# The convolution branch's output projection by seven products of quarters, with its operand's sums formed earlier

## The chip, the cores and the metric

The kernel is one launch on one core of a Trainium2 chip. The metric is the device time of that launch in microseconds (us), the median of several runs; lower is better. The engines are named as in the profile: PE is TensorE, which multiplies matrices, and PEld its loading of weights; DVE is VectorE; ACT is ScalarE; POOL is GpSimd and SP is SyncE, which here do little besides issuing DMA transfers. SBUF is the memory on the core, PSUM the eight banks that the matmuls write to, DRAM the memory off the core.

## The reference

One layer of a hybrid decoder in float32, with 512 tokens, width 2048, 1024 convolution channels, 1024 attention channels in 8 heads, and a hidden width of 8192:

```python
h = rmsnorm(x, g_mix)
z = h @ w_in                          # conv B | C | V, attn Q | K | V, forget, gate conv, gate attn
conv_y = cb * causal_dwconv(cc * cv, conv_w)          # 512 x 1024
conv_branch = conv_y @ w_conv_out                     # 512 x 2048
attn_branch = forgetting_attention(q, k, v, log_f) @ w_attn_out
merged = sigmoid(gate_c + b) * conv_branch + sigmoid(gate_a + b) * attn_branch
x = x + merged @ w_mix_out
h = rmsnorm(x, g_mlp)
x = x + square(relu(h @ w_ff1)) @ w_ff2
out = rmsnorm(x, g_final)
```

The change concerns the product that makes `conv_branch`.

## The kernel before

Every float32 operand is split in two: `hi`, which ACT copies into the type that PE multiplies (L100), and `lo`, the rest, which DVE subtracts (L101). A product is then three matmuls: hi by hi, hi by lo, lo by hi.

The large projections do with seven products of quarters what plainly takes eight (the Strassen-Winograd scheme): `Group` (L170 to L312) cuts the operands into quarters A11, A12, A21, A22, forms sums of the other operand S1 to S4 once for all groups, and sums of the weights for each group by `sub` (L104). `whole` runs the products A11, A12, S1, S3, S2, S4, A22 in this order into PSUM banks a, b, a, c, d; `snap` (ACT) copies a bank into a tile `o`, `plus` (DVE, L107) adds another bank to it, and `put` stores the result. A matmul there is 128x128 by 128x256. A product has six matmuls for each tile of 128 rows that the quarter has in depth: 48 in a group of `w_in`. A group's last argument, `extra`, puts a surplus matmul of 192 columns at the head of a named product: "first" (L137) or in a spare bank (L631).

The work up to the end of attention and its place in time: the columns of `w_in` for K, Q and V come first, then six z groups (the convolution's B, C and V, stored in DRAM as `z_d`), the first four among the attention heads. The last two z groups start at 482.1 and 521.1 us. `conv_job(f)`, for f from 0 to 7, loads three rows of `z_d`, forms u = C V and the three taps on DVE (L616, L619, L621, L622) and stores the result as `y_d` from POOL; DVE works on them from 474.6 to 602 us, in between the instructions of the groups. Eight gates groups follow on PE, up to 867.5 us; they store sigmoids of gates in `g_d`. `yact` and `aact` (`split_from`) load `y_d` and `a_d` (attention's output) and split them into SBUF.

The output projections come next, in `gemm_t` (L334): for a block c of 512 columns, conv with `yact`, then attn with `aact`, for c from 0 to 3. Each loads 1 MB of weights twice, splits them, and runs 96 matmuls of 128x128 by 128x512 into four banks, `pt`; `cons_cv` multiplies a bank by its gate into `held`, `cons_at` does so with the other, adds `held`, and splits the sum into `M`, the operand of mix_out, which follows at 1041.6 us. Then come ff1 (1222 to 1830 us) and ff2 (to the end).

What stands in an engine's queue is decided when the program is built: each engine runs its instructions in one fixed order, and an instruction that waits holds up all behind it. SP's and POOL's queues of DMA issues behave the same. Small tiles of the stage `pb` (`at`) share six buffers of 128x512; tiles `o` five; weights of groups four slots x0 to x3; `th` and `tl` (the split weights) two each.

Of the kernel before, what the change touches and what calls it, by code (L numbers as in the profile page):

```python
# [20 lines left out]
HS = S // 2  # L21
CW = D // 2
CT = CW // P
# [14 lines left out]
WBUF, SHIFT, PAD = 33 * 64, 16, 16  # L38
# [7 lines left out]
def tile_hybrid_block(ctx: ExitStack, tc, x, g_mix, w_in, b_f, b_gate, conv_w, w_conv_out,  # L46
                      w_attn_out, w_mix_out, g_mlp, w_ff1, w_ff2, g_final, out):
    nc = tc.nc
    x, out = x[0], out[0]
    w_in, w_conv_out, w_attn_out, w_mix_out = w_in[0], w_conv_out[0], w_attn_out[0], w_mix_out[0]  # L50
# [25 lines left out]
    z_d = dram.tile([3, CT, P, S], F32, name="z_d")  # L76
    g_d = dram.tile([2, KT, P, S], F32, name="g_d")
    y_d = dram.tile([CT, P, S], F32, name="y_d")
    a_d = dram.tile([CT, P, S], F32, name="a_d")
    x1_d = dram.tile([NT, P, D], F32, name="x1_d")  # L80
    s_d = [dram.tile([P, 2, 4, 7, HS], F32, name=f"s_d{i}") for i in range(DFF // 1024)]
# [17 lines left out]
    def split(src, hi, lo):  # L99
        nc.scalar.activation(out=hi, in_=src, func=AF.Copy)  # L100
        nc.vector.tensor_tensor(out=lo, in0=src, in1=hi.bitcast(F32), op=ALU.subtract)  # L101

    def sub(out, a, b):
        nc.vector.tensor_tensor(out=out, in0=a, in1=b, op=ALU.subtract)  # L104

    def add(out, a, b):
        nc.vector.tensor_tensor(out=out, in0=a, in1=b, op=ALU.add)  # L107
# [58 lines left out]
    def moving(t):  # L166

        return lambda q: (t[:, 0, q, :], t[:, 1, q, :])


    free, later = [0, 1, 2, 3], []

    class Group:
# [3 lines left out]
        def __init__(self, view, c1, c2, w, ST, mm, banks, put, scale=1.0, extra={}):  # L177
            self.extra = extra
            self.view, self.cs, self.w, self.ST, self.mm, self.banks = view, (c1, c2), w, ST, mm, banks
            self.put, self.scale, self.at = put, scale, {}  # L180

        def load(self, i, j):

            t = main.tile([P, KT // 2, self.w], F32, tag=f"x{free[0]}", name=f"x{i}{j}")
# [7 lines left out]
            return [bank(i, which) for i in self.banks["abcd".index(which)]]  # L192

        def run(self, ps, n, src, first):
            hi, lo = parts([P, KT // 2, self.w], SHIFT if self.w == HS else 0)
# [28 lines left out]
        def done(self, *ij):  # L224
            free.append(self.at.pop(ij))
# [90 lines left out]
    def eights(t, w=S):  # L316

        return tuple(t[:, e].rearrange("p (k s) -> p k s", s=w) for e in range(2))
# [11 lines left out]
    def slot(slots):  # L330
        turns[0] += 1
        return slots[turns[0] % len(slots)]

    def gemm_t(view, kt, c0, act, banks, consume, slots=(0, 3, 2)):  # L334

        ps = [bank(i, "pt") for i in banks]
        for k0 in range(0, kt, 4):
            hi, lo = wchunk(view, k0, c0, slot(slots))
            for j in range(4):
                js = slice(j * P, (j + 1) * P)  # L340
                for q in range(4):
                    k = k0 + q
                    xh, xl = act(k)
                    nc.tensor.matmul(ps[j], hi[:, q, js], xh, start=k == 0, stop=False)
                    nc.tensor.matmul(ps[j], hi[:, q, js], xl, start=False, stop=False)  # L345
                    nc.tensor.matmul(ps[j], lo[:, q, js], xh, start=False, stop=k == kt - 1)
        for j in range(4):
            consume(j, ps[j])
# [30 lines left out]
    class Quarters:  # L379
# [20 lines left out]
        def put(self, n, src, ts=slice(0, HS)):  # L400
            split(src[:, :, ts], self.ST[n][:, 0, :, ts], self.ST[n][:, 1, :, ts])
# [33 lines left out]
    ph = ExitStack()  # L435
# [3 lines left out]
    for t in range(NT):  # L439
        h = xp[t // 2][:, t % 2]  # L440
        n = 4 if t == 0 else 2
# [59 lines left out]
    def whole(g):  # L501
        g.head(True)
        g.tail2()
# [106 lines left out]
    def conv_job(f):  # L610
        cv, cc, cb = at("cv"), at("cc"), at("cb")
        for k, t in enumerate((cb, cc, cv)):
            nc.sync.dma_start(out=t, in_=z_d[k, f])
        u = at("u", [P, S + 2])
        nc.gpsimd.memset(u[:, 0:2], 0.0)
        nc.vector.tensor_tensor(out=u[:, 2:], in0=cv, in1=cc, op=ALU.mult)  # L616
# [5 lines left out]
        nc.vector.tensor_tensor(out=y, in0=cb, in1=y, op=ALU.mult)  # L622
        nc.gpsimd.dma_start(out=y_d[f], in_=y)
# [22 lines left out]
    for f in range(CT):  # L646
        conv_job(f)

    for f in range(0, KT, 2):
        def put_g(i, j, v, f=f):  # L650
            for b in range(2):
# [5 lines left out]
                    extra=apart(4, "S2", 0)))  # L657
# [21 lines left out]
    M = {}  # L679
    M[0, 0], M[0, 1], M[1, 0] = (eights(pair(i, F32R, "m"), HS) for i in (4, 5, 6))  # L680
    M[1, 1] = eights(pc_.tile([P, 2, D], F32R, tag="h", name="m"), HS)
    for c in range(4):
        held = main.tile([P, 4, S], F32, tag="x1", name="held")

        def gate(k, j, c=c):
            t = otile([P, S], "gt")
            nc.sync.dma_start(out=t, in_=g_d[k, 4 * c + j])
            return t

        def cons_cv(j, ps, held=held, gate=gate):  # L690
            g = gate(0, j)
            nc.vector.tensor_tensor(out=held[:, j, :], in0=ps, in1=g, op=ALU.mult)

        def cons_at(j, ps, held=held, gate=gate, c=c):
            g = gate(1, j)
# [174 lines left out]
    held = []  # L870
# [305 lines left out]
```

## Time and profile before

| | |
|---|---|
| median of 3 runs | 2461.55 us (2460.36 to 2463.54) |
| the profiled execution's own time | 2459.11 us |
| its span in the trace | 2457.4 us |
| granted clock of PE, mean | 0.998 |
| PE busy | 2431.6 us, 99% of the span, 16928 matmuls |
| PEld busy | 2247.3 us, 91% |
| DVE busy | 1921.1 us, 78% |
| ACT busy | 1149.1 us, 47% |
| POOL busy | 180.0 us, 7% |
| output projections (tile `pt`) | 867.5 to 1041.6 us |

The page has the span in us; its groups give busy time and the mean duration of one instruction in ns. A row of the trace by tile or line gives minimum, median and maximum duration in ns, the first and last start in us and the shapes. Durations of successive instructions on an engine overlap, so the distance between their starts is what counts for a sum.

### The profile page before, as it was taken

To read this page: it belongs to the slowest core of one execution; us is meant where nothing else is said; L and a number is where in the kernel's file an instruction comes from. 1 tells how busy PE (TensorE), PEld (TensorE's weight loads), DVE (VectorE), ACT (ScalarE), POOL (GpSimd) and SP (SyncE) were. 2 spreads that over 40 slices of the span, in tenths; PEclk is the share of its full clock that TensorE was granted. 3 is DMA by queue.
4 is the path that set the end of the run, shared out by engine and by line. 5 is a ranking of instruction groups with operands and counts; after the bars stand their busy time and mean duration, and the time that the engine had idled before them with its cause. 6 is when DMAs were issued, how large, how long until landed. Compare 5 with 4: busy or idle time off the path is not lost.

```text
span 2457.4 us, 39283 instructions
## 1 busy us (share of the span) xinstructions
PE 2431.6 (99%) x16928; PEld 2247.3 (91%) x16928; DVE 1921.1 (78%) x1592; ACT 1149.1 (47%) x1147; POOL 180.0 (7%) x280
## 2 busy tenths in 40 slices
PE   8999999999999999999999999999999999999998
PEld 8999999999999988888899999999998888888886
DVE  7887777788777744425688898988988888889898
ACT  6443443334444532225556666666665333333334
POOL 0100000001000000000000000000011001100000
PEclk9999999999999999999999999999999999999999
DMA  7564544456534554335645646556488576655662
GB/s 249 182 191 143 165 128 138 155 168 210 163 118 149 176 180 142 128 137 190 204 144 202 237 178 228 198 201 235 172 298 299 169 253 223 239 187 184 246 224 102
DMA packets 272036, 463.00 MB, mean 188 GB/s; under 512 B 10269, under 2 KB 172181, under 8 KB 271733
## 3 DMA queue, kind: packets, MB, share of 16 engines
q1 hardware_dynamic: 235136, 303.13, 38.3%
q0 software_dynamic: 35856, 156.25, 16.9%
q8 instruction: 133, 2.18, 0.4%
q10 hardware_dynamic: 868, 1.10, 0.1%
q14 instruction: 43, 0.34, 0.0%
HBM read 368.16 MB, written 92.27 MB: 187 GB/s over the span
## 4 chain that ended last, share of the span: by engine, by line
PE 95%; DVE 3%; issue 1%; ACT 1%; DMA 1%; POOL 0%; SPq 0%; DVEq 0%; POOLq 0%; ACTq 0%
PE a L148 6%; PE a L144 6%; PE a L146 6%; PE a L162 5%; PE a L164 5%; PE a L161 5%; PE d L148 5%; PE d L144 5%; PE d L146 5%; PE c L146 4%; PE c L144 4%; PE c L148 3%; PE d L162 3%; PE d L164 3%; PE d L161 3%; PE b L144 2%
## 5 line engine op out<-in xcount | busy, mean ns | idle before, releaser
L100 ACT ACTIVATE th<-x 128x2048 fp32r<-128x2048 f32 (+1 forms) x252 | 483.2, 1918 | 506.3 <-DVE x L104 156.5
L101 DVE TENSOR_TENSOR tl<-x,th 128x2048 fp32r<-128x2048 f32 (+1 forms) x252 | 575.6, 2290 | 172.1 <-ACT th L100 157.9
L104 DVE TENSOR_TENSOR x<-x,x 128x2048 f32<-128x2048 f32 (+1 forms) x144 | 329.7, 2289 | 8.3 <-DMA x<-in_w_in_dram 6.2
L100 ACT ACTIVATE th<-y 128x2048 fp32r<-128x2048 f32 x81 | 155.6, 1922 | 227.7 <-PE a L162 138.7
L101 DVE TENSOR_TENSOR tl<-raw,th 128x2048 fp32r<-128x2048 f32 x40 | 91.7, 2293 | 150.7 <-ACT th L100 150.1
L161 PE MATMUL a<-th,us 128*128 128x512 f32 x512 | 199.2, 389 | 0.0
L162 PE MATMUL a<-th,us 128*128 128x512 f32 x512 | 199.2, 389 | 0.0
L101 DVE TENSOR_TENSOR tl<-y,th 128x2048 fp32r<-128x2048 f32 x81 | 185.1, 2288 | 16.8 <-ACT th L100 16.6
L144 PE MATMUL a<-ST,th 128*128 128x256 f32 x752 | 173.4, 277 | 0.8 <-ACT th L100 0.8
L146 PE MATMUL a<-ST,th 128*128 128x256 f32 x752 | 172.9, 276 | 0.0
L100 ACT ACTIVATE th<-raw 128x2048 fp32r<-128x2048 f32 x40 | 76.7, 1918 | 176.3 <-PE pt L345 71.5
L144 PEld LDWEIGHTS a<-ST,th 128*128 128x128 f32 x752 | 141.2, 188 | 1.1 <-ACT th L100 1.0
L146 PEld LDWEIGHTS a<-ST,th 128*128 128x128 f32 x752 | 141.2, 188 | 0.0
L164 PE MATMUL a<-tl,us 128*128 128x512 f32 x512 | 136.7, 389 | 0.0
L144 PE MATMUL c<-S,th 128*128 128x256 f32 x576 | 134.6, 278 | 0.0
L146 PE MATMUL c<-S,th 128*128 128x256 f32 x576 | 134.4, 278 | 0.0
L100 ACT ACTIVATE th<-t 128x2048 fp32r<-128x2048 f32 x31 | 59.5, 1919 | 125.3 <-DVE t L104 73.0
L144 PE MATMUL d<-ST,th 128*128 128x256 f32 x512 | 117.7, 276 | 0.0
L146 PE MATMUL d<-ST,th 128*128 128x256 f32 x512 | 117.6, 276 | 0.0
L162 PEld LDWEIGHTS a<-th,us 128*128 128x128 f32 x512 | 96.1, 188 | 20.0
L164 PEld LDWEIGHTS a<-tl,us 128*128 128x128 f32 x512 | 96.0, 188 | 20.0
L161 PEld LDWEIGHTS a<-th,us 128*128 128x128 f32 x512 | 96.1, 188 | 20.0
(298 smaller groups left out, 6384.0 us busy)
## 6 DMA issues: line engine op xcount, KB each, us to landing
x<-in_w_in_dram SPq DMA_DIRECT2D x86, 1024.0 KB, 5.7
x<-in_w_ff_dram SPq DMA_DIRECT2D x64, 1024.0 KB, 7.2
y<-in_w_ff_dram SPq DMA_DIRECT2D x64, 1024.0 KB, 7.7
us<-s_d POOLq DMA_DIRECT2D x48, 1024.0 KB, 9.0
s_d<-rh POOLq DMA_DIRECT2D x32, 896.0 KB, 5.6
s_d<-r POOLq DMA_DIRECT2D x32, 896.0 KB, 5.8
raw<-in_w_mix_out_dram SPq DMA_DIRECT2D x24, 1024.0 KB, 5.1
g_d<-o POOLq DMA_DIRECT2D x32, 256.0 KB, 2.7
```

The source lines that it names most:

```text
L100: nc.scalar.activation(out=hi, in_=src, func=AF.Copy)
L101: nc.vector.tensor_tensor(out=lo, in0=src, in1=hi.bitcast(F32), op=ALU.subtract)
L104: nc.vector.tensor_tensor(out=out, in0=a, in1=b, op=ALU.subtract)
L144: nc.tensor.matmul(o, hi[:, q, js], Sh, start=first and q == 0 and j == 0, stop=False, skip_group_check=True)
L146: nc.tensor.matmul(o, hi[:, q, js], Sl, start=False, stop=False, skip_group_check=True)
L148: nc.tensor.matmul(o, lo[:, q, js], Sh, start=False, stop=q == nq - 1, skip_group_check=True)
L161: nc.tensor.matmul(o, Sh, hi[:, q, :], start=begin and q == 0, stop=False, skip_group_check=True)
L162: nc.tensor.matmul(o, Sl, hi[:, q, :], start=False, stop=False, skip_group_check=True)
L164: nc.tensor.matmul(o, Sh, lo[:, q, :], start=False, stop=q == nq - 1, skip_group_check=True)
```

## The change

The convolution's output projection is made by `whole` too, as a `Columns(Group)` with its own loads. Its depth is 1024, so a quarter has four tiles and a product 24 matmuls of 128x128 by 128x256; each of the four blocks c takes 7 x 24 = 168 and two surplus matmuls of 192 columns, at A11 and S3, in the place of 96 of 128x512. The attention half keeps `gemm_t`. The order of the eight is conv 0, attn 0, conv 1, attn 1, conv 2, conv 3, attn 2, attn 3. The product of block 3 with its gate goes to DRAM (`held_d`) and is loaded again before attn 3.

The moving operand's sums S1 to S4 and their hi and lo parts are made in `sums_job(q)`, after every second `conv_job`. Such a job loads two tiles of `y_d`, forms four sums of 128x256, splits 256 + 512 + 512 + 512 columns and stores hi and lo as `ys_d` by eight DMAs on POOL. The parts come back by eight loads on POOL where `yact` was split before. Gates of the convolution half are loaded on POOL, four to a block, in the place of SP's `gt` loads.

```diff
+    ys_d = dram.tile([P, 2, CT // 2, 7, HS], F32, name="ys_d")
+    held_d = dram.tile([4, P, S], F32, name="held_d")
...
+    def sums_job(q):
+        even, odd = at("even"), at("odd")
+        for t, f in ((even, 2 * q), (odd, 2 * q + 1)):
+            nc.sync.dma_start(out=t, in_=y_d[f])
+        a11, a21, a12, a22 = even[:, :HS], even[:, HS:], odd[:, :HS], odd[:, HS:]
+        s13, s24 = at("s13"), at("s24")
+        add(s13[:, :HS], a21, a22)
+        sub(s13[:, HS:], a11, a21)
+        sub(s24[:, :HS], s13[:, :HS], a11)
+        sub(s24[:, HS:], a12, s24[:, :HS])
+        for t, n, w in ((even, 0, HS), (odd, 1, S), (s13, 3, S), (s24, 5, S)):
+            h = at("hi", dt=F32R)
+            split(t[:, :w], h[:, :w], t[:, :w])
+            for e, o in enumerate((h.bitcast(F32), t)):
+                nc.gpsimd.dma_start(out=ys_d[:, e, q, n:n + w // HS], in_=o[:, :w].rearrange("p (n s) -> p n s", s=HS))
     for f in range(CT):
         conv_job(f)
+        if f % 2:
+            sums_job(f // 2)
...
-    yact = split_from(y_d, (0, 1))
+    for place, names, first in ((0, ("A11", "A12"), 0), (1, ("S1", "S3"), 3), (5, ("S2", "S4"), 5)):
+        load_y(main.tile([P, 2, CT // 2, 2, HS], F32R, tag=f"t{place}", name="ys"), names, first)
     aact = split_from(a_d, (2, 3))
...
+    def conv_out(c, banks):
+        gates = {}
+        for i, j in ((0, 0), (1, 1), (0, 1), (1, 0)):
+            gates[i, j] = pc_.tile([P, 2, HS], F32, tag="hg", name="gates", bufs=4)
+            k = 4 * c + 2 * j
+            nc.gpsimd.dma_start(out=gates[i, j], in_=g_d[0, k:k + 2, :, i * HS:(i + 1) * HS].rearrange("k p s -> p k s"))
...
+        def put(i, j, v):
+            ts = slice(i * HS, (i + 1) * HS)
+            o = held[c][:, 2 * j:2 * j + 2, ts] if c < 3 else v
+            nc.vector.tensor_tensor(out=o, in0=v, in1=gates[i, j], op=ALU.mult)
+            if c == 3:
+                nc.gpsimd.dma_start(out=held_d[2 * j:2 * j + 2, :, ts].rearrange("k p s -> p k s"), in_=o)
+        whole(Columns(w_conv_out, c * S, c * S + HS, HS, YS.get, mm_cols, tuple((b,) for b in banks), put,
+                      extra={"A11": "first", "S3": "first"}))
...
-        gemm_t(w_conv_out, CT, c * S, yact, range(4), cons_cv)
-        gemm_t(w_attn_out, CT, c * S, aact, range(4, 8), cons_at)
+    for c in (0, 1):
+        conv_out(c, lower)
+        attn_out(c, upper)
+    conv_out(2, lower)
+    conv_out(3, upper)
...
+    attn_out(2, lower)
+    attn_out(3, upper)
```

The change also moves what stands in the queues. The first place is DVE in the z group that starts at 482.1 us, from the addition of bank b (`o<-b`) to that of bank c (`o<-c`). Before, with `x01`, `x10`, `x11` the group's weights, `tl` their lo parts, and `u` and `y` the tiles of `conv_job`:

```order
L107 TENSOR_TENSOR o_5235<-b_5237,o_5235 128x512
L101 TENSOR_TENSOR tl_5353<-x01_5292,th_5352 128x2048
L621 SCALAR_TENSOR_TENSOR y_6015<-u_6012,cols_94,y_6015 128x512
L104 TENSOR_TENSOR x01_5292<-x11_5294,x00_5177 128x2048
L622 TENSOR_TENSOR y_6015<-cb_6008,y_6015 128x512
L104 TENSOR_TENSOR x10_5179<-x10_5179,x01_5292 128x2048
L101 TENSOR_TENSOR tl_5409<-x01_5292,th_5408 128x2048
L616 TENSOR_TENSOR u_6027<-cv_6021,cc_6022 128x512
L101 TENSOR_TENSOR tl_5467<-x11_5294,th_5466 128x2048
L107 TENSOR_TENSOR o_5405<-c_5297,o_5405 128x512
```

The same stretch now, with `even` and `odd` the two tiles loaded from `y_d`:

```order
L109 TENSOR_TENSOR o_5237<-b_5239,o_5237 128x512
L103 TENSOR_TENSOR tl_5355<-x01_5294,th_5354 128x2048
L106 TENSOR_TENSOR s13_6012<-even_6008 128x256
L106 TENSOR_TENSOR x01_5294<-x11_5296,x00_5179 128x2048
L109 TENSOR_TENSOR s13_6012<-even_6008,odd_6009 128x256
L106 TENSOR_TENSOR x10_5181<-x10_5181,x01_5294 128x2048
L103 TENSOR_TENSOR tl_5411<-x01_5294,th_5410 128x2048
L106 TENSOR_TENSOR s24_6013<-s13_6012,even_6008 128x256
L106 TENSOR_TENSOR s24_6013<-odd_6009,s24_6013 128x256
L103 TENSOR_TENSOR tl_5469<-x11_5296,th_5468 128x2048
L109 TENSOR_TENSOR o_5407<-c_5299,o_5407 128x512
```

The taps of the next `conv_job` have left this stretch, and four sums of 128x256 stand between the weights' instructions; the second of them needs the load of `odd`.

The second place is SP's queue ahead of the first gates group (before, then now), whose weights are the `x` tiles:

```order
L613 DMA cb<-z_d 128x512
L613 DMA cc<-z_d 128x512
L613 DMA cv<-z_d 128x512
L188 DMA x_6620<-in_w_in_dram 128x8x256
L188 DMA x_6622<-in_w_in_dram 128x8x256
```

```order
L653 DMA even<-y_d 128x512
L191 DMA x_6626<-in_w_in_dram 128x8x256
L191 DMA x_6628<-in_w_in_dram 128x8x256
L191 DMA x_6742<-in_w_in_dram 128x8x256
L653 DMA odd<-y_d 128x512
L191 DMA x_6744<-in_w_in_dram 128x8x256
```

The load of `odd`, which waits for the store of `y_d`, now stands ahead of the last of the group's four weight loads.

The third place is DVE in conv 0, from the addition of bank b to that of bank c (`y0`, `y1` are the halves of its weights, `a` to `d` its banks); before, the four `held<-pt,gt` products of 128x512 and the splits of the next weights are all that stands there:

```order
L103 TENSOR_TENSOR tl_9607<-y0_9535,th_9606 128x1024
L109 TENSOR_TENSOR o_9568<-b_9570,o_9568 128x512
L103 TENSOR_TENSOR tl_9637<-y1_9601,th_9636 128x1024
L743 TENSOR_TENSOR held_9534<-o_9568,gates_9526 128x2x256
L106 TENSOR_TENSOR y1_9601<-y1_9601,y0_9535 128x1024
L106 TENSOR_TENSOR y0_9535<-y0_9535,y1_9601 128x1024
L103 TENSOR_TENSOR tl_9670<-y1_9601,th_9669 128x1024
L103 TENSOR_TENSOR tl_9703<-y1_9601,th_9702 128x1024
L109 TENSOR_TENSOR o_9666<-c_9605,o_9666 128x512
```

In the order of the products, the three `tl` in the middle belong to S3, S2 and S4, and the subtraction `y1<-y1,y0` makes the weights of S2. The product with the gate stands between them.

More of the change, by code (lines that the diff above doesn't have):

```diff
@@ L180, in __init__ @@
             self.put, self.scale, self.at = put, scale, {}
+            self.nq = view.shape[0] // (2 * P)
         def load(self, i, j):
-            t = main.tile([P, KT // 2, self.w], F32, tag=f"x{free[0]}", name=f"x{i}{j}")
+            t = main.tile([P, self.nq, self.w], F32, tag=f"x{free[0]}", name=f"x{i}{j}")
             self.at[i, j] = free.pop(0)
@@ L194, in run @@
         def run(self, ps, n, src, first):
-            hi, lo = parts([P, KT // 2, self.w], SHIFT if self.w == HS else 0)
+            hi, lo = parts([P, self.nq, self.w], SHIFT if self.w == HS else 0)
             split(src, hi, lo)
@@ L672, in split_from, with load_y @@
         return lambda k: tuple(e[:, k % 4, :] for e in r[k // 4])
-    yact = split_from(y_d, (0, 1))
+    YS = {}
+    def load_y(t, names, at):
+        for e in range(2):
+            nc.gpsimd.dma_start(out=t[:, e].bitcast(F32), in_=ys_d[:, e, :, at:at + len(names)])
+        for e, n in enumerate(names):
+            YS[n] = moving(t[:, :, :, e])
+    for place, names, first in ((0, ("A11", "A12"), 0), (1, ("S1", "S3"), 3), (5, ("S2", "S4"), 5)):
+        load_y(main.tile([P, 2, CT // 2, 2, HS], F32R, tag=f"t{place}", name="ys"), names, first)
     aact = split_from(a_d, (2, 3))
@@ L678, in tile_hybrid_block @@
     pc_ = ph.enter_context(phase("pc"))
[L679 to L687, printed above, removed]
-            return t
[L690 to L695, printed above, removed]
+    load_y(pc_.tile([P, 2, CT // 2, 1, HS], F32R, tag="y22", name="ys"), ("A22",), 2)
@@ new lines, in tile_hybrid_block, with load, done @@
+    class Columns(Group):
+        def load(self, i, j):
+            if (1 - i, j) not in self.at:
+                self.at[i, j] = main.tile([P, 2, self.nq, self.w], F32, tag=f"x{slot((0, 3, 2))}", name=f"y{j}")
+            else:
+                self.at[i, j] = self.at[1 - i, j]
+            t, c = self.at[i, j][:, i], self.cs[j]
+            src = self.view[:, c:c + self.w].rearrange("(q two p) c -> two p q c", two=2, p=P)
+            nc.sync.dma_start(out=t, in_=src[i])
+            return t
+        def done(self, *ij):
+            self.at.pop(ij)
@@ new lines, in tile_hybrid_block @@
+    M, held = {}, {}
+    def conv_out(c, banks):
[4 more added lines that the diff above has]
+            nc.gpsimd.dma_start(out=gates[i, j], in_=g_d[0, k:k + 2, :, i * HS:(i + 1) * HS].rearrange("k p s -> p k s"))
+        if c < 3:
+            held[c] = main.tile([P, 4, S], F32, tag="x1", name="held")
+        def put(i, j, v):
[6 more added lines that the diff above has]
+                      extra={"A11": "first", "S3": "first"}))
@@ L696, in cons_at, with attn_out @@
+    def attn_out(c, banks):
+        if c == 3:
+            held[c] = main.tile([P, 4, S], F32, tag="x1", name="held")
+            nc.sync.dma_start(out=held[c], in_=held_d.rearrange("k p s -> p k s"))
+        def cons_at(j, ps, held=held[c], c=c):
+            g = otile([P, S], "gt")
+            nc.sync.dma_start(out=g, in_=g_d[1, 4 * c + j])
             nc.vector.tensor_tensor(out=g, in0=ps, in1=g, op=ALU.mult)
@@ L701, in cons_at @@
                 split(g[:, p * HS:(p + 1) * HS], hi[:, k % 8, :], lo[:, k % 8, :])
-        gemm_t(w_conv_out, CT, c * S, yact, range(4), cons_cv)
-        gemm_t(w_attn_out, CT, c * S, aact, range(4, 8), cons_at)
+        gemm_t(w_attn_out, CT, c * S, aact, banks, cons_at)
+    lower, upper = range(4), range(4, 8)
+    M[0, 0], M[1, 0] = (eights(pair(i, F32R, "m"), HS) for i in (4, 6))
+    for c in (0, 1):
[3 more added lines that the diff above has]
+    conv_out(3, upper)
+    M[0, 1] = eights(pair(5, F32R, "m"), HS)
+    ph.close()
+    ph = ExitStack()
+    pc_ = ph.enter_context(phase("pm"))
+    M[1, 1] = eights(pc_.tile([P, 2, D], F32R, tag="h", name="m"), HS)
+    attn_out(2, lower)
+    attn_out(3, upper)
     ss2 = const.tile([P, NT, 5], F32, name="ss2")
```

## The prediction

> **What bounds the kernel now.** I read the page first: its busy times, and the chain of work that ended last.
>
> ```profile
> PE 2431.6 (99%) x16928; PEld 2247.3 (91%) x16928; DVE 1921.1 (78%) x1592; ACT 1149.1 (47%) x1147; POOL 180.0 (7%) x280
> PE 95%; DVE 3%; issue 1%; ACT 1%; DMA 1%; POOL 0%; SPq 0%; DVEq 0%; POOLq 0%; ACTq 0%
> ```
>
> PE has no idle time worth the name, and the chain runs along it. Matmuls taken out therefore shorten the span by their spacing, unless DVE, ACT or a transfer then comes last. The two stages that the change touches are compared by the windows of the trace; x is the number of instructions.
>
> ```profile
> core 0: us, PE busy (x) PEld busy (x) DVE busy (x) ACT busy (x) POOL busy (x), PEclk, DMA share, GB/s
> 477.30:636.20 158.90, 158.88 (x1374) 158.65 (x1374) 135.85 (x103) 68.07 (x57) 16.73 (x31) 1.00 0.61 195
> 590.00:620.00 30.00, 30.00 (x257) 30.00 (x257) 29.47 (x24) 14.08 (x15) 4.09 (x7) 1.00 0.67 230
> 640.00:670.00 30.00, 30.00 (x267) 30.00 (x266) 21.41 (x13) 13.88 (x15) 1.46 (x2) 1.00 0.41 127
> 867.50:1041.60 174.10, 174.10 (x771) 144.14 (x770) 79.18 (x95) 41.65 (x49) 0.73 (x1) 1.00 0.45 151
> 950.00:1000.00 50.00, 50.00 (x222) 41.42 (x221) 25.24 (x35) 13.86 (x18) 0.00 (x0) 1.00 0.47 156
> ```
>
> The stretch from 477.3 to 636.2 us holds all convolution jobs. DVE is busy there for 135.85 of 158.90 us, and from 590 to 620 for 29.47 of 30. There the new sums go. The projections (867.5 to 1041.6 us) leave DVE more than half idle.
>
> **What the seven products save.** Rows of the tile `pt`, and the surplus matmul of 192 columns:
>
> ```profile
> L344 PE MATMUL pt<-act,th x256: 389/389/395, 867.5 to 1040.9; 128*128 128x512 f32 x128
> L346 PE MATMUL pt<-act,tl x256: 389/389/389, 867.9 to 1041.3; 128*128 128x512 f32 x128
> L631 PE MATMUL spare<-S,th x10: 248/248/352, 504.0 to 851.0; 128*128 128x192 f32 x10
> ```
>
> Three such lines of 256 make 768 matmuls, from 867.5 to 1041.5 us: 174.0 / 768 = 0.2266 us each. The conv half is 384 of them, 87.0 us. In its place come 4 x 168 = 672 matmuls of 256 columns. The windows give their spacing: 267 in 30 us from 640 on, 0.1124, and half of 0.2266 is 0.1133; a few counted at the edges make the difference, and I take 0.1133. That is 76.1 us, and 8 surplus ones at 192/256 of it 0.7. The conv half is then 76.8 us: **-10.2 us** on PE.
>
> The spacing isn't always that. From 590 to 620 us only 257 fit, 30 / 257 = 0.1167, with PE and PEld both shown busy throughout at a granted clock of 1.00. By it the 672 take 78.4 us and the saving is 7.9: the upper end. PEld is busy 41.42 of 50 us at 512 columns and 30.00 of 30 at 256, so short matmuls leave the weight loads no room. The page "TensorE: Matmul & The Clock Gate" of the Trainium skill, in "Back-to-back issue gap", has the spacing set by both operations, with 81 ns at 128 columns and 131 ns at 512. An estimate from that page puts 256 columns near 98 ns, three quarters of the 512 price, by which the seven products would cost some 27 us more than the direct ones. The window of 267 matmuls disagrees with that, and decides.
>
> **What DVE and ACT do for it in the projections.** Prices of shapes, by line:
>
> ```profile
> L101 DVE TENSOR_TENSOR tl<-x,th x252: 2268/2291/2326, 26.9 to 1827.2; 128x2048 fp32r<-128x2048 f32 x123, 128x2080 fp32r<-128x2080 f32 x3
> L101 DVE TENSOR_TENSOR A<-h,A x6: 1216/1219/1223, 17.8 to 39.2; 128x1024 fp32r<-128x1024 f32 x6
> L100 ACT ACTIVATE A<-h x6: 1041/1050/1063, 16.4 to 37.2; 128x1024 fp32r<-128x1024 f32 x6
> L101 DVE TENSOR_TENSOR act<-raw,act x16: 681/685/687, 837.4 to 869.0; 128x512 fp32r<-128x512 f32 x16
> L101 DVE TENSOR_TENSOR m<-gt,m x32: 416/419/427, 906.4 to 1046.1; 128x256 fp32r<-128x256 f32 x32
> L692 DVE TENSOR_TENSOR held<-pt,gt x16: 683/692/693, 882.6 to 1020.0; 128x512 f32<-128x512 f32 x16
> ```
>
> A conv group takes seven splits and four sums of 128x1024 at 1.22 us, five additions at 0.685 and four gate products at 0.69: 13.4 + 3.4 + 2.8 = 19.6 us of DVE to 19.2 us of PE. Successive instructions overlap by some 0.08 us, which brings DVE to about 18. Alternating with attn it has 21.8 us of PE's time more, for some 14 us of work. So conv 0 and conv 1 are covered; conv 3, right behind conv 2, is the tight one. Inside a group one chain matters: bank b's addition (0.69), S3's lo part (1.22), the gate product (0.69), the subtraction for S2 (1.22), then ACT's hi part of S2 (1.05), 4.9 us, while PE runs S1 and S3, 2 x 24 x 0.1133 = 5.4 us. About 0.5 us is left, some of it lost between engines. I count 0.3 us for conv 1, 0.7 for conv 3 and nothing else: **+1 us**. The bounds are 0 (the slack holds everywhere) and 3 (0.7 us in every group). Loads of operands and gates from DRAM are priced by the nearest ones (KB, us to landing):
>
> ```profile
> us<-s_d POOLq DMA_DIRECT2D x48, 1024.0 KB, 9.0
> gt<-g_d SPq DMA_DIRECT2D x32, 256.0 KB, 3.8
> ```
>
> The operands' loads can be issued while the gates groups still run, and conv 0's first gate is used some 7 us after the last gate was stored; `held` comes back while attn 2 runs, 22 us. I cost them at nothing; without that cover a gate load costs up to its 3.8 us once. ACT has 19 us of PE time for 7 x 1.05 and four snaps, and doesn't bind. The 8 splits of `yact` that go lie before 867.5 us, where DVE has time, and give nothing back.
>
> **What the sums cost.** A sums job is four sums and a split of 256 columns and three splits of 512: 5 x 0.42 + 3 x 0.685 = 4.2 us, four jobs 16.6 us. DVE in their stretch goes from 135.85 to 152.5 of 158.9 us. POOL gets 8 issues for a job, SP two. The dearer part is the waits at the head of DVE's queue: each job reads `y_d` right after it was stored.
>
> ```profile
> y_d<-y POOLq DMA_DIRECT2D x8, 256.0 KB, 4.3
> raw<-y_d SPq DMA_DIRECT2D x8, 256.0 KB, 5.0
> cv<-z_d SPq DMA_DIRECT2D x8, 256.0 KB, 3.7
> DMA to landing us min/median/max: 2.3/4.8/9.0
> ```
>
> The last column is us to landing; the last row is that of stores and loads of `y_d` together. Now the place where the first job goes in DVE's timeline before, with POOL's store first (start, duration):
>
> ```profile
> 493.91 0.57 POOL L623 DMA_DIRECT2D y_d<-y  x1 [0.80 <-DVE y L622]
> 492.92 0.69 DVE L622 TENSOR_TENSOR y<-cb,y 128x512 f32<-128x512 f32 x1
> 495.50 0.69 DVE L107 TENSOR_TENSOR o<-b,o 128x512 f32<-128x512 f32 x1
> 496.10 2.28 DVE L101 TENSOR_TENSOR tl<-x,th 128x2048 fp32r<-128x2048 f32 x1
> 501.76 2.29 DVE L104 TENSOR_TENSOR x<-x,x 128x2048 f32<-128x2048 f32 x1
> 503.96 2.29 DVE L101 TENSOR_TENSOR tl<-x,th 128x2048 fp32r<-128x2048 f32 x1
> 508.97 0.69 DVE L107 TENSOR_TENSOR o<-c,o 128x512 f32<-128x512 f32 x1
> 515.74 2.29 DVE L101 TENSOR_TENSOR tl<-x,th 128x2048 fp32r<-128x2048 f32 x1 [0.58 <-ACT th L100]
> ```
>
> The second tile's store, issued at 493.9, lands at 498.2; its load takes 3.7 to 5.0 us more with 0.3 for the issue: 501.9 to 503.2. A step of 128x2048 takes 2.2 us from start to start (501.76 to 503.96). DVE, in its new order, ends S3's lo part at 498.3, one sum at 498.6 and the 2048 subtraction at 500.8, and waits there 1.1 to 2.4 us. Then come a sum (0.34), a subtraction (2.2), S2's lo part (2.2), two sums (0.7) and S4's lo part (2.2) before the addition of bank c, whose bank S4 needs on PE: 7.6 us on, at 509.5 to 510.8 in the place of 508.97. The job costs PE 0.5 to 1.8 us here; I take 0.5, by the loads of `z_d`. Behind it the next `u` takes one of the six `at` buffers, which come free when the job's stores have landed. The splits end near 512.3, POOL issues eight times 0.57, and the store that counts lands near 518; so the lo part that stands at 515.74 ends some 4 us later, and the next group's A12, after two subtractions, has its lo part about 1 us late.
>
> The same walk gives 3.1 us for job 1, whose second tile is loaded late between weight loads, just ahead of the first gates group (1.4 at S2's lo part, 1.7 at S4's); 2.1 at S2's for job 2; nothing for job 3. That is 6.7 us in all. But PE already loses time here: the row of the 192-column matmul, one in each of ten groups, has nine group lengths from 504.0 to 851.0, 347.0 us, where 9 x (336 x 0.1133 + 0.09) is 343.4. The 3.6 us are lost by slow spacing, almost all of it ahead of 640 us, and where PE waits for an operand that DVE and DMA bring, slow spacing ahead of it costs nothing more. I let 2.7 of the 6.7 coincide: **+4 us**. The bounds are 1, nearer to how the trace treats such waits so far, and 8, by a reload of 5.0 us each time.
>
> ```profile
> DVE u L616 <- DMA cv<-z_d: 2.8, 2, 2.5
> PEld c L144 <- DVE o L107: 0.2, 1, 0.2
> ```
>
> These are waits from 477 to 640 us (total, times, longest). DVE has already stood 2.8 us for rows of `z_d`, and PE waited 0.2 us in all.
>
> By the page "DMA: Bandwidth & Descriptors" of the Trainium skill ("Anatomy of one DMA — SWDGE (gpsimd) path") a transfer costs about 2.0 us and its bytes at 436 GB/s. An estimate by that is 2.6 us for 256 KB, a round trip of 5.2 us in the place of 8 to 9.3, and the sums would then cost 1 us or less. The landings of 4.3 and 5.0 us above are longer, and I go by them.
>
> **The sum**, against the profiled execution: 2459.11 - 10.2 + 1 + 4 = 2453.9 us. That execution lies 2.44 us under the median of the runs, so 2456.4 us is what I expect of the median. A measurement of this kernel can tell about 0.2%, 4.9 us, from no change: below 2456.6 is faster, above 2466.5 slower. My forecast stands on the border.
>
> **The rivals.**
>
> A, the waits are hidden. The trace's 0.2 us of PE waiting in 163 us speaks for it, DVE at 96% of the stretch against. Then only the conv stage's 1 us is paid: 2459.11 - 9.2 + 2.44 = 2452.3 us.
>
> B, the sums' round trips become the bound, on the other side. Its place is the three jobs that precede job 3, its price what a landing takes beyond the 5.0 us used above. With the 9.0 us of the longest row each costs 4 us more, 12 in all: 2456.4 + 12 = 2468.4 us. Slower than the border needs 10 us, 3.4 us a job. For it speaks that DMA carries 0.61 to 0.67 of its share here, more than in later groups; against it that the median is 4.8.
>
> C, the weight loads bound the short matmuls in the conv groups, which run at 0.1167 us as from 590 to 620: 2.3 us more, 2458.7 us. The surplus matmuls and short halts could start it. The gates from 640 on, at 0.1124, speak against it. (The skill's rule quoted above is this mechanism at a higher price; no window here bears that price out.)
>
> That the change doesn't do what it says can be excluded: 384 matmuls of 512 columns are gone from PE's queue and 680 shorter ones stand there.
>
> **Chances and range.** The forecast has 0.45, A 0.25, B 0.18, C 0.12. Faster by over 0.2%: A's 0.25 and half of the forecast, 0.23, 0.48. Slower: B, 0.18. Within: the rest, 0.34. The forecast's own bounds are 2459.11 - 10.2 + 1 + 2.44 = 2452.4 and 2459.11 - 10.2 + 11 + 2.44 = 2462.4. The range reaches below A by a microsecond, for the spread of the runs, and above the forecast's bound toward B: 2451 to 2465.
>
> **What would show it.** Right: the conv matmuls of 256 columns spaced 0.113 us; PE waits of 0.5 to 3 us for S2's or S4's parts in the z and first two gates groups, with DVE's sum waiting for `odd` ahead of them; the gates' second group starting about 4 us late; 1 us of gaps in the projections, and mix_out starting some 5 us earlier than 1041.6. Wrong: PE gaps at conv 0's entry, where operands come from DRAM; a stage after mix_out that changes by more than 1 us; sums' waits over 5 us; or a spacing of 0.117 us or more through the conv groups.

## The result and the profile after

The changed kernel takes 2475.07 us (median of 4 runs, 2473.27 to 2477.30), the kernel before 2461.13; the ratio is 1.0059, with a 95% interval of 1.0047 to 1.0071. It is 14 us slower, where 2456.4 with a range of 2451 to 2465 was forecast. The profiled execution took 2474.6 us, its span is 2472.9.

PE's busy time shrank by 4.1 us, from 2431.6 to 2427.5, where 10.2 was forecast (matmuls at a lowered clock, see below, count as busy too). In other places it stands idle now. The page's busy times:

```profile
PE 2427.5 (98%) x17224; PEld 2254.5 (91%) x17224; DVE 1974.2 (80%) x1672; ACT 1173.9 (47%) x1191; POOL 217.8 (9%) x340
```

Where it stands idle is read from the starts of the stages: the surplus matmul of 192 columns ahead of each of the last two z groups (`a<-A`) and of each conv group (`a<-ys`), and the first matmuls of mix_out (`pn`). The first row is the kernel before, the others are the changed one.

```profile
L137 PE MATMUL a<-A,th x2: 252/252/253, 482.1 to 521.1; 128*128 128x192 f32 x2
L139 PE MATMUL a<-A,th x2: 248/248/248, 481.6 to 519.9; 128*128 128x192 f32 x2
L139 PE MATMUL a<-ys,th x4: 248/250/252, 883.9 to 992.3; 128*128 128x192 f32 x4
L354 PE MATMUL pn<-th,m x256: 389/389/477, 1056.6 to 1236.3; 128*128 128x512 f32 x128
```

From the fifth z group to the projections it is 883.9 - 481.6 = 402.3 us, before 867.5 - 482.1 = 385.4: **16.9 us more**. The projections take 1056.6 - 883.9 = 172.7 us, before 174.1: 1.4 less, where 9.2 less was forecast. What follows mix_out is unchanged within a microsecond. The windows of the changed kernel by stage:

```profile
core 0: us, PE busy (x) PEld busy (x) DVE busy (x) ACT busy (x) POOL busy (x), PEclk, DMA share, GB/s
477.30:652.10 174.80, 162.22 (x1390) 160.44 (x1388) 145.49 (x131) 73.79 (x71) 31.36 (x59) 0.99 0.63 207
652.10:700.00 47.90, 46.12 (x400) 45.72 (x401) 40.14 (x25) 26.02 (x30) 7.06 (x11) 1.00 0.62 210
700.00:883.90 183.90, 183.90 (x1625) 183.90 (x1624) 133.84 (x82) 90.69 (x96) 18.28 (x25) 1.00 0.54 173
883.90:909.70 25.80, 21.65 (x172) 21.29 (x171) 18.28 (x19) 12.18 (x15) 6.55 (x9) 0.93 0.57 185
909.70:1056.60 146.90, 146.32 (x897) 129.93 (x896) 106.09 (x132) 53.59 (x72) 10.12 (x14) 1.00 0.50 171
```

PE was idle for 12.6 us among the sums jobs (to 652.1), 1.8 us in the group after, nothing from 700 on, and 4.2 us in conv 0 alone, where a group should take 19.2 us and took 25.8. DVE has 29 us without work in the first of these windows: it is not full, it waits. The idle time is 14.4 of the 16.9 us; behind the longest wait the clock cost PE another 1.6, as it was granted at 0.62 for 4.2 us:

```profile
533.70:537.90 4.20, 4.20 (x24) 4.20 (x25) 4.17 (x5) 1.87 (x1) 0.57 (x1) 0.62 0.22 66
```

What PE waited for (total, times, longest), from 515 to 662 us:

```profile
PE spare L634 <- ACT th L102: 5.3, 2, 2.7
PE b L150 <- DVE tl L103: 2.7, 1, 2.7
PE c L150 <- DVE tl L103: 1.9, 1, 1.9
PE b L146 <- ACT th L102: 1.6, 1, 1.6
```

And what DVE waited for, from 478 to 690 us:

```profile
DVE u L619 <- DMA cv<-z_d: 10.8, 3, 4.2
DVE s L109 <- DMA odd<-y_d: 8.9, 3, 4.5
DVE tl L103 <- ACT th L102: 8.0, 5, 2.8
DVE s L103 <- ACT hi L102: 7.1, 4, 2.6
```

PE's operands were late because DVE's in-order queue stood at three kinds of instruction that none of the groups needs: `u` of a convolution job, waiting for a row of `z_d` (2.8 us before), the sum that needs `odd`, and the splits of the sums, waiting for ACT. The first such wait shows the chain. SP's issues of a convolution job's loads, then DVE:

```profile
515.03 0.62 SPq L616 DMA_DIRECT2D cc<-z_d  x1
516.92 0.32 SPq L616 DMA_DIRECT2D cv<-z_d  x1
...
515.94 0.68 DVE L109 TENSOR_TENSOR o<-a,o 128x512 f32<-128x512 f32 x1
520.84 0.69 DVE L619 TENSOR_TENSOR u<-cv,cc 128x512 f32<-128x512 f32 x1 [4.21 <-DMA cv<-z_d]
```

The rows of `z_d` had been in DRAM for long. What SP waited for, from 478 to 690 us, begins so:

```profile
SPq L653 <- DMA y_d<-y: 55.3, 8, 10.7
SPq L191 <- DVE x L106: 42.7, 6, 24.2
SPq L191 <- DVE tl L103: 37.7, 9, 8.6
SPq L616 <- DMA ys_d<-even: 16.8, 2, 10.6
```

L616 are the loads of the convolution jobs: they waited until a buffer of the six was free, that is until a store of the sums job had landed, and `cv` landed another 3.9 us after its issue. DVE, with `u` next in its order, did nothing for 4.2 us, and the second z group paid for it.

### The profile page after: what moved, and what is told of

Its sections match the earlier page's. It is cut to its first block, busy times and chain, and to the rows that moved or that the text cites. A ratio compares the mean times of both kernels' runs of the same rounds, so it can differ in the third digit from the quotient of the medians.

```text
span 2472.9 us, 40195 instructions
## 1 busy us (share of the span) xinstructions
PE 2427.5 (98%) x17224; PEld 2254.5 (91%) x17224; DVE 1974.2 (80%) x1672; ACT 1173.9 (47%) x1191; POOL 217.8 (9%) x340
## 4 chain that ended last, share of the span: by engine, by line
PE 68%; DVE 2%; DMA 1%; issue 1%; ACT 1%; POOL 0%; DVEq 0%; POOLq 0%; ACTq 0%
PE a L166 5%; PE a L163 5%; PE a L164 5%; PE a L146 4%; PE a L148 4%; PE a L150 4%; PE d L146 3%; PE d L150 3%; PE d L148 3%; PE d L163 2%; PE d L166 2%; PE d L164 2%; PE c L146 2%; PE c L148 2%; PE c L150 2%; PE pn L354 2%
## 5 line engine op out<-in xcount | busy, mean ns | idle before, releaser
L102 ACT ACTIVATE th<-y 128x2048 fp32r<-128x2048 f32 (+1 forms) x109 | 184.8, 1700 | 274.0 <-PE a L164 137.6
L103 DVE TENSOR_TENSOR tl<-y,th 128x2048 fp32r<-128x2048 f32 (+1 forms) x109 | 218.9, 2013 | 33.6 <-ACT th L102 31.6
L103 DVE TENSOR_TENSOR tl<-raw,th 128x2048 fp32r<-128x2048 f32 x32 | 73.4, 2292 | 99.5 <-ACT th L102 99.2
L102 ACT ACTIVATE th<-raw 128x2048 fp32r<-128x2048 f32 x32 | 61.4, 1918 | 100.8 <-PE pn L356 42.4
```

## The experiments

Profiles of different kernels differ by up to 6 us in where the fifth z group starts (481.6 to 487.6 us), though the program's text ahead of it is the same. So I give two lengths beside each median: **A**, from the start of the fifth z group to that of the projections (before 385.4, changed 402.3), and **B**, the projections (174.1 and 172.7), both from rows like the three above. The medians of before in these runs were 2460.7 to 2461.6 us.

**The sums without the new projections.** `sums_job` and `ys_d` added to the kernel before:

```diff
     for f in range(CT):
         conv_job(f)
+        if f % 2:
+            sums_job(f // 2)
```

> The kernel before, with the four sums jobs and their stores added; nothing reads what they store, and the projections stay direct. Read from the changed kernel's trace, the z and gates groups lost 16.5 us up to the projections. If the sums jobs alone cause that, this kernel is 16 us (14 to 18) slower than before, about 2477 us. If the loss needs the new projections too (their loads, their order), it is under 8 us.

Measured: 2481.87 us, ratio 1.0090 (1.0075 to 1.0105); A is 891.2 - 487.6 = 403.6. The jobs alone cost 18 us in A, the projections have no part in it. (The median lies higher than the changed kernel's, since B keeps its 174.1 and its fifth z group started 6.0 us later.)

**The seven products without the sums.** The operand's loads read rows of `z_d`:

```diff
-        if f % 2:
-            sums_job(f // 2)
...
-            nc.gpsimd.dma_start(out=t[:, e].bitcast(F32), in_=ys_d[:, e, :, at:at + len(names)])
+            src = z_d[e, :4] if len(names) == 2 else z_d[e, 4:, :, :HS]
+            nc.gpsimd.dma_start(out=t[:, e].bitcast(F32), in_=src.rearrange("k p (n s) -> p k n s", s=HS))
```

> The changed kernel without the sums jobs: the conv projection's operands are loaded from rows of z_d, of the same sizes and at the same places, so its products are those of other numbers. Theory: the seven products save 10.2 us, conv 0's entry costs 6.6 us as in the changed kernel's trace (first gate's load late behind the last group's splits, then a slow clock), conv 3 about 1: 2.4 us faster than before, about 2459 us. Rival: conv 0's entry is late only because the sums made everything late; then 8 to 9 us faster, about 2452.5.

What this kernel leaves out is the sums, so its `conv_branch` is not the layer's. Measured: 2457.31 us, ratio 0.9991 (0.9982 to 1.0000); A 383.6, B 172.1. Conv 0 took 893.9 - 868.5 = 25.4 us, so its loss is its own and not handed on by the sums.

**The stores taken away.** The first experiment's kernel without the two DMAs of each split:

```diff
             h = at("hi", dt=F32R)
             split(t[:, :w], h[:, :w], t[:, :w])
-            for e, o in enumerate((h.bitcast(F32), t)):
-                nc.gpsimd.dma_start(out=ys_d[:, e, q, n:n + w // HS], in_=o[:, :w].rearrange("p (n s) -> p n s", s=HS))
```

> The kernel before with the sums jobs' loads, sums and splits but without their stores (nothing reads the sums). With the stores it took 2481.9 us, 21 more than before. Theory of held buffers: a job's eight small tiles are free as soon as DVE has read them, so the next convolution job's loads are no longer late: at most 5 us over before, about 2466. Theory of DVE's work (16.6 us added on the engine) or of the wait for the second tile's load: both are still there, 12 us or more over before.

Measured: 2469.32 us, ratio 1.0029 (1.0017 to 1.0042); A 392.9. Between the two expectations: the stores are worth 10.7 us of the 18.2 in A, the rest stays at 7.5. DVE's waits from 478 to 690 us have shrunk for `cv` and for `odd`, and not gone:

```profile
DVE s L108 <- DMA odd<-y_d: 5.8, 3, 4.6
DVE u L617 <- DMA cv<-z_d: 5.8, 3, 3.1
```

**The stores alone.** The loaded tiles are stored, eight DMAs a job, without sums and splits:

```diff
-        add(s13[:, :HS], a21, a22)
...
-            split(t[:, :w], h[:, :w], t[:, :w])
+        for t, n, w in ((even, 0, HS), (odd, 1, S), (even, 3, S), (odd, 5, S)):
+            for e in range(2):
+                nc.gpsimd.dma_start(out=ys_d[:, e, q, n:n + w // HS], in_=t[:, :w].rearrange("p (n s) -> p n s", s=HS))
```

> The kernel before with the jobs' loads and eight stores each, but without the sums and splits (the loaded tiles themselves are stored). Theory of held buffers: two of the six small buffers are held until the last of eight stores lands, some 12 us a job, so that a part of the loss is there without any work on DVE: 4 to 12 us over before. Theory of DVE's work: under 2 us.

Measured: 2470.54 us, ratio 1.0038 (1.0025 to 1.0051); A 881.2 - 486.5 = 394.7, 9.3 over before. Loads and stores cost over half of the loss without a cycle of work on DVE, whose waits were (478 to 690 us)

```profile
DVE u L617 <- DMA cv<-z_d: 13.3, 4, 7.6
```

Neither theory holds alone. By A the stores are worth some 9 to 11 us, the sums and splits with their waits 7 to 9, and 9.3 + 7.5 is nearly the 18.2. But the two runs do not separate the theories cleanly. SP's waits (478 to 690 us; first row the stores alone, second row the kernel without stores) show that the loads of the convolution jobs (L614) waited for a buffer in both, in the first until a store had landed and in the second until a split was done, so held buffers have a part in the 7.5 too:

```profile
SPq L614 <- DMA ys_d<-odd: 10.0, 2, 6.1
SPq L614 <- DVE odd L102: 9.2, 2, 8.1
```

And part of each length is the clock. The kernel with sums and stores ran 13.9 us behind its waits at a granted clock of 0.51, in three stretches of which the first is shown:

```profile
539.50:546.40 6.90, 6.19 (x29) 6.19 (x30) 6.79 (x9) 1.91 (x1) 0.57 (x1) 0.51 0.35 114
```

Without the stores it was 3.6 us at 0.53, with the stores alone 3.5 us at 0.51. PE's busy time there times what the clock lacks makes an estimate of 6.4, 1.7 and 1.7 us; less these, the 18.2, 7.5 and 9.3 are some 12, 6 and 8.

**The jobs emitted later.** The four calls after gates groups 2 to 5 in the program's text:

```diff
+        if f in (4, 6, 8, 10):
+            sums_job((4, 6, 8, 10).index(f))
```

> The changed kernel with the four sums jobs after gates groups 2, 3, 4 and 5, where no convolution job follows them. If the loss came from small buffers that the jobs hold until their stores have landed, so that the next convolution job's loads and with them DVE's queue stand still, 14 us or more of the 16.5 go: about 2460 us. If DVE's added work of 16.6 us is what costs, these groups with DVE 76% busy keep 4 to 8 us of it: about 2464 to 2467. Conv 0's 6.6 us should stay in either case.

Measured: 2469.70 us, ratio 1.0036 (1.0023 to 1.0048); A 393.8, a gain of 8.5, short of both figures for the buffers. The jobs did not go where the text put them: their sums stand at 611 to 660 us, one behind the other,

```profile
L109 DVE TENSOR_TENSOR s<-even,odd x4: 417/419/425, 611.5 to 659.7; 128x256 f32<-128x256 f32 x4
```

right after the convolution jobs, four times 4.2 us of work and 32 stores in 60 us. So this one doesn't tell the theories apart; it shows that the place in the text alone did not move the work into later groups.

**One job to a group.** The loads are made to wait for the last output of gates group q + 2 by a copy of one column:

```diff
-    def sums_job(q):
+    def sums_job(q, v):
         even, odd = at("even"), at("odd")
+        for t in (even, odd):
+            nc.vector.tensor_copy(t[:, :1], v[:, 0, :1])
...
+            if (i, j) == (1, 0) and f // 2 in (2, 3, 4, 5):
+                sums_job((2, 3, 4, 5).index(f // 2), v)
```

> The changed kernel with sums job q tied to the last output of gates group q + 2 (a copy of one column makes its loads wait for it), so that one job goes into each of four groups, with no convolution job behind. The work on DVE is the same. Both theories expect a gain; held buffers at its most, 13 to 16 us under the changed kernel (2459 to 2462); if DVE's queue in a gates group has no room for 4.2 us and a wait for the loads, 4 us a group stay and the gain is near nothing. Conv 0's 6.6 us stay.

Measured: 2459.07 us, ratio 0.9989 (0.9980 to 0.9999); A 867.9 - 484.5 = 383.4. That is 16.0 us under the changed kernel, the upper end of what held buffers expect: the loss in A is gone, with the same work and the same stores. The four jobs' sums now start between 685.5 and 800.7 us. DVE's waits for loads of the jobs, from 478 to 868 us, and the only wait of PE there:

```profile
DVE u L619 <- DMA cv<-z_d: 3.8, 3, 2.5
DVE s L106 <- DMA even<-y_d: 1.0, 3, 0.4
PE c L146 <- DVE o L109: 0.5, 1, 0.5
```

Now conv 0, which B is left with. In the changed kernel, POOL's queue, then DVE, then the windows (PE's busy time first, the clock third from the end), and last what SP waited for with the loads of the attention operand (860 to 892 us):

```profile
888.29 1.52 POOL L700 DMA_DIRECT2D ys<-ys_d  x2 [5.62 <-DVE o L109]
889.80 0.72 POOL L676 DMA_DIRECT2D g_d<-o  x1
890.52 2.88 POOL L736 DMA_DIRECT2D gates<-g_d  x4
...
884.91 1.33 DVE L103 TENSOR_TENSOR act<-raw,act 128x512 fp32r<-128x512 f32 x2 [1.93 <-ACT act L102]
887.30 0.68 DVE L109 TENSOR_TENSOR o<-d,o 128x512 f32<-128x512 f32 x1
896.55 0.69 DVE L743 TENSOR_TENSOR held<-o,gates 128x512 f32<-128x512 f32 x1 [3.43 <-DMA gates<-g_d]
897.15 2.48 DVE L106 TENSOR_TENSOR y<-y,y 128x1024 f32<-128x1024 f32 x2
...
897.00:899.50 2.50, 0.00 (x0) 0.00 (x0) 2.47 (x3) 1.01 (x2) 0.72 (x1) 1.00 0.31 92
899.70:903.40 3.70, 3.70 (x19) 3.70 (x20) 2.84 (x3) 1.52 (x3) 0.00 (x0) 0.54 0.12 29
...
SPq L691 <- DVE act L103: 6.4, 2, 6.3
```

The gates' loads were issued 6.6 us after the group's start, behind the load of A22, and landed 6.0 us later. The gate product stood ahead of the subtraction that makes S2's weights, and PE waited 3.0 us. When it went on, the granted clock was 0.54 for 3.7 us. And the last two splits of the attention operand (884.91), whose loads wait for one of the same six buffers, stood ahead of `o<-d`, which empties the bank that A12 needs.

**The gate product put later.** The first `put` of a conv group goes into the list that the tail runs behind S2's snap:

```diff
+            if (i, j) == (0, 0) and not again:
+                later.append(lambda: put(i, j, v, True))
+                return
```

> The changed kernel, with the first gate product of each conv group put behind the snap of S2, so that the subtraction for S2's weights no longer stands behind the load of the gate on DVE. If that order is the cause at conv 0, its 3.0 us wait and the 2.4 us at half clock behind it go: 5 us (4 to 6) under the changed kernel, about 2470 us. If the operands from DRAM or DVE's splits of the attention operand hold conv 0, under 1.5 us.

Measured: 2478.39 us, 3 more than the changed kernel. It tests nothing: in DVE's built order the product (897.64 us) still stands ahead of the subtraction (898.25). A is 400.9 and B 171.2, 2.9 less together than in the changed kernel; the fifth z group started 2.1 us later, and what follows B took 4.0 us more. Of these 4.0 more than half is matmul spacing: from 1270 to 1330 us, in ff1, which the edit doesn't touch, 512 matmuls ran where the changed kernel ran 532, 20 x 0.113 = 2.3 us (the first row is this kernel's):

```profile
1270.00:1330.00 60.00, 60.00 (x512) 60.00 (x512) 50.67 (x39) 35.76 (x37) 2.75 (x5) 1.00 0.50 173
1270.00:1330.00 60.00, 60.00 (x532) 60.00 (x531) 52.28 (x40) 35.86 (x38) 2.77 (x6) 1.00 0.53 184
```

**The first block's gates on SP.**

```diff
-            nc.gpsimd.dma_start(out=gates[i, j], in_=...)
+            (nc.sync if c == 0 else nc.gpsimd).dma_start(out=gates[i, j], in_=...)
```

> The changed kernel with the first block's four gate loads issued on SP instead of POOL, where they stood behind the last operand load and the last store of gates. If that queue made the first gate late, it lands about 4 us earlier, the 3 us wait for S2 and the slow clock behind it go: 4 to 5 us under the changed kernel, about 2470.5. If the stage's memory, which both loads need, comes free too late, or the transfers' crowding makes the landing late, less than 1.5 us.

Measured: 2476.43 us, no gain in the median; A 401.4, B 1055.9 - 887.1 = 168.8, 3.9 less than the changed kernel's, against 4 to 5 expected. The wait for S2 is gone; of conv 0's waits on PE only A12's is left:

```profile
PE b L146 <- DVE o L109: 2.0, 1, 2.0
```

In the profiled execution the gain is hidden by what the edit doesn't touch: the fifth z group started 4.1 us later (485.7 us), and the part behind B took 1.6 us more.

**Spread sums and gates on SP.** Both edits above.

> Both edits together: one sums job in each of gates groups 3 to 6, and the first block's gate loads on SP. Of the 5.0 us that conv 0's entry still lost in the spread version's trace, the wait for A12 (2.4, a bank that an addition empties late) should stay and the one for S2 (2.4) go: 2 to 3 us under the spread version, about 2456.5 us, which is 5 us under before. If the gate's queue doesn't matter, 2459.

Measured: 2456.47 us, ratio 0.9983 (0.9974 to 0.9992); A 382.2, B 167.4. It is 2.6 us under the spread version, and B is 3.8 shorter; 0.9 of the 2.6 is a difference of the two sets of runs, in which the kernel before took 2460.7 and 2461.6 us. The wait for S2 is gone, as expected. The wait for A12, which was to stay at 2.4 us, is 0.8; why is open, so that the size came out right in part by luck.

**The last two splits later too.** The splits of the attention operand from the seventh on are made behind conv 0, and their loads go to tiles `o`:

```diff
+                if 4 * i + k < 6:
+                    part(at("raw"))
+                else:
+                    rest.append(part)
...
         conv_out(c, lower)
+        while rest:
+            rest.pop(0)(otile([P, S], "raw"))
         attn_out(c, upper)
```

> The same, and the last two of the eight splits of the attention operand put behind conv 0, with buffers of the tiles o for their loads, so that they no longer wait for one of the six small buffers ahead of the last gates group's additions. If these two splits hold both the bank that A12 needs and the gates' place in memory, conv 0's entry loses under 1 us: 4 to 5 us under the spread version, about 2454.5 us. Rival: the loads then stand in the way of conv 1's weights or attn 0, and it gains nothing on the version without this.

Measured: **2451.14 us**, ratio 0.9966 (0.9953 to 0.9978), 9.6 us under before; A 383.2, B 165.7. That is 7.9 us under the spread version, more than expected; B explains 5.5 of it (171.2 there), the two sets of runs 0.9. Conv 0 and what follows it have no gap left:

```profile
866.60:885.80 19.20, 19.20 (x172) 19.20 (x171) 15.99 (x17) 9.87 (x12) 2.49 (x4) 1.00 0.67 217
885.80:1032.20 146.40, 146.36 (x896) 130.07 (x895) 107.43 (x134) 54.48 (x73) 10.12 (x14) 1.00 0.52 179
```

**The same with the gates on POOL.**

> The spread sums and the two late splits, with all gate loads on POOL as in the changed kernel. If the two splits are the root of both waits, this alone takes most of conv 0's 5 us: about 2455 us. If POOL's queue is a cause of its own, the wait for S2 stays and it is 2457.

Measured: 2452.47 us, ratio 0.9966 (0.9954 to 0.9977); A 382.8, B 166.4. PE's only wait from 478 to 1033 us is one in conv 3 (at 980.6 us):

```profile
PE a L146 <- ACT th L102: 0.6, 1, 0.6
```

With the two splits out of the way POOL's queue costs conv 0 nothing: against the spread version the edit moves only these two splits, and both of conv 0's waits are gone with them (B 4.8 less). The splits, where they stood and with the buffers they used, were the root of both.

## Why the prediction was wrong

- **The seven products' saving, -10.2 us: right.** Conv 0 in the last version but one takes the 19.2 us that 168 matmuls at 0.1133 and two surplus ones make, and that version's B is 8.4 us under before, where the saving less the 1 us of the next point makes 9.2.
- **Conv 1 to 3, +1 us: right.** The chain through S3, the gate product and S2 held in all of them but conv 3, and from 909.7 to 1056.6 us PE was idle for 0.6 of 146.9 us. Rival C has no part: conv 1 and conv 2 took 19.3 us each, which is 0.113 us a matmul. The 27 us that were estimated from the page "TensorE: Matmul & The Clock Gate" of the Trainium skill ("Back-to-back issue gap") did not come.
- **Operands and gates from DRAM at conv 0, costed at nothing: wrong, 6.6 us.** The working had the cover (some 7 us) and a price for one load, 3.8 us once. It left out what is queued ahead of that load: on POOL the load of A22 and the last store of gates, which needs an addition on DVE, behind two splits that wait for small buffers. The load itself took 6.0 us. Behind the wait came some half of the clock (0.54 for 3.7 us). The gap at conv 0's entry is the first of the prediction's own signs of being wrong.
- **The sums, +4 us with bounds of 1 and 8: the step that failed, with 16.9 us.** Several parts of it went wrong. The walk let the next `u` run when the job's stores had landed, near 518 us; but what waits for the free buffer is the *load* of `cv`, which takes 3.9 us more, so that `u` began at 520.84, and this was priced once, at 1 us, where DVE met it three times. And 2.7 us were taken off because slow spacing would be hidden; of some 13 products at the slow spacing in this stretch 6 were left, which hid 1.6, and the lowered clock behind a wait, which had no price, took as much back.
- **The waits for `odd`, in the same step: at the wrong jobs.** SP's queue that is shown as the change's second place stands ahead of the second gates group, not the first (in the trace `even` at 586.4 us, three weight loads, `odd` at 601.3, the fourth at 601.7; that group starts at 607.9): it is job 2's. DVE waited 0.7 us for `odd` in job 0, nothing in job 1, 4.5 in job 2 and 3.7 in job 3, which the walk had free. (For job 0 the walk names 0.3 us for the issue of a load and leaves it out of the sum that gives 501.9 to 503.2; the sum that needs `odd` ran at 499.64.)
- **Rival B had the sign and the price** (16 us of sums, 2468), **and the wrong mechanism**, so the price is luck. It needed landings of 9 us. The round trips were shorter than assumed:

```profile
y_d<-y POOLq DMA_DIRECT2D x8, 256.0 KB, 2.4
odd<-y_d SPq DMA_DIRECT2D x4, 256.0 KB, 2.9
```

DVE waited 8.9 us for `odd` all the same, as its load was issued late: SP stood at weight loads that wait for a slot, or at the store. Here the short estimate from the page "DMA: Bandwidth & Descriptors" of the Trainium skill ("Anatomy of one DMA — SWDGE (gpsimd) path"; 5.2 us a round trip, with 5.3 measured) was nearer than the medians of before. The section is on transfers that POOL issues, and the load of `odd` is issued by SP, so half of that agreement is not the page's. The conclusion drawn from it, 1 us or less, was farthest off.
- **Rival A is refuted** for this placement by 16.9 us in A, and borne out for another: with one job to a gates group, DVE's 16.6 us left PE with 0.5 us of waiting in all of A.

That the place of the sums jobs among the convolution jobs costs the 17 to 18 us in A is shown: the jobs alone bring the loss, and the same jobs in later groups don't. How much of it each of the held buffers, the late `odd` and DVE's work make is open beyond the two parts that were taken away singly. Buffers of the jobs' own, which would settle it, were not tried.

## What to carry to other kernels

An engine with an in-order queue and idle time is not free for more work: look at what the added instructions wait for, and what the needed ones behind them then cost. A store out of a rotating buffer holds that buffer until it lands, and the next user is a load that takes its own landing time on top; count both, for every round. Put work that needs memory round trips into a stretch where nothing else shares its buffers, tie it there by a dependence, since its place in the text did not decide here, and look at what stands ahead of the first use at the entry of each stage.

## What the runs showed of the hardware

After a gap PE may come back at half speed. In the changed kernel PE waited 3.0 us for S2 in conv 0, with no matmul from 897.0 to 899.5 us, and then had a granted clock of 0.54 from 899.7 to 903.4, which cost S2 1.7 us beside the wait. The page "TensorE: Matmul & The Clock Gate" of the Trainium skill ("What's actually happening") ties the low clock to an idle window of about 3.4 us; the gap here is shorter, with another of 1.2 us some 9 us ahead. Two other waits of the same kernel, 2.7 us each, went differently: behind the one that ended at 533.6 us the clock was 0.62 for 4.2 us, behind the one that ended at 590.7 it was 1.00.

Matmuls of 256 columns run at two spacings at a clock of 1.00, 532 or 512 in 60 us of ff1, and which stretches are slow changes between kernels whose code there is the same. No run here shows what causes it. With what happens ahead of the fifth z group (6 us between profiles) it sets how small an edit a single median of this kernel can show; the length of a stage in the trace tells more. It is in these lengths too: counted from the starts of the matmuls, spacing wider than 0.1133 us took 3.3 us of A in the kernel before and 0.7 in the spread version, which is why the latter's A is the shorter one by 2.0.
